# A gate projection's first two chunks made directly instead of by seven products

## The chip, the cores and the metric

One core of a Trainium2 chip runs the whole kernel. What counts is the device time of one execution in microseconds (us). Engines are named as in the profile: PE is TensorE, DVE is VectorE, ACT is ScalarE, POOL is GpSimd, SP is SyncE, which only issues transfers here.

## The reference, cut to what matters

An encoder block over 1024 tokens and 16 meta tokens of width 1024. The normalised input is projected by `w_in` to ten groups of columns. Two attention branches follow, each gated by `silu` of one group (`za`, `zb`) and projected by its own matrix. The last two groups, `ga` and `gb`, are 1024 columns each and are the subject here:

```python
proj = hn @ w_in[layer] + b_in[layer]
qa, ka, va, za, qb, kb, vb, zb, ga, gb = jnp.split(proj, SPLITS, axis=-1)
...
ya = (oa * jax.nn.silu(za)) @ w_out_a[layer]
yb = (ob * jax.nn.silu(zb)) @ w_out_b[layer]
mixed = jax.nn.sigmoid(ga) * ya + jax.nn.sigmoid(gb) * yb
h = h + rmsnorm(mixed @ w_out[layer], post_norm_g[layer])
```

All is float32. The kernel keeps that precision by splitting every operand into a high and a low part and adding three products: high by high, high by low, low by high.

## The kernel before

**Direct projection.** The normalised input lies transposed in four tiles: `hn00` and `hn01` are the high parts of the first and of the second half of the tokens, `hn10` and `hn11` the low parts. `proj` (lines 143 to 157) makes a chunk of 128 columns for two halves of 512 tokens: 24 matmuls of 128x512 for each half (8 slices of the width, three products), so 48 for a chunk. Its weights come by `load_w` (lines 121 to 141) in four pieces of two slices each: a load of 128 KB on SP's queue into a tile `wr`, a copy to the high part `wh` on POOL (line 139), and a subtraction for the low part `wl` on POOL (line 140).

**Seven products.** For `ga` and `gb` the input is cut into quarters, b11 and b21 (halves of the width for the first tokens), b12 and b22 (for the second tokens), and two chunks of columns are made together from seven products instead of eight (`seven`, lines 857 to 900). A product P1 to P7 is 12 matmuls of 128x512. P1, P2 and P3 use quarters as they are; P6, P5, P4 and P7 use the sums t2, t1, t4 and t3 of quarters. The weights of P5, P6, P3 and P7 are sums of weight blocks too, made on DVE (`total`, line 863, tiles `ws`). Every product's weights are split by `split` (lines 816 to 818): the high part on ACT, the low part on POOL. DVE adds the products up (line 897). The order is P1, P2, P6, P5, P3, P7, P4 (`SEVEN`).

**The sums of the input's quarters.** `combos` (lines 820 to 855) makes t1, t2, t4 and t3 in halves (f1, f2, f4, f3): two or three long DVE additions each, then a split, ACT for the high part and POOL for the low part. t3 is written over the quarter b12, so its split is a step of its own at the end of `combos`. Before that step eight steps run while the four chunks of `za` are projected directly (line 936), two with each chunk (lines 933 and 934). The last step is taken by `between`, ahead of P6 of the first pair of `ga`.

**Beside it.** `gate_a` (lines 905 to 914) gates the first branch in the `za` chunks: a sigmoid on ACT and DVE's lines 910 and 911, then a store of the result `ga_d`. `gate_b` (lines 916 to 923) gates the second branch, once for each pair of `ga`: loads of `zb_d` and `ob_d` on SP's queue, a sigmoid on ACT, two multiplications on DVE (lines 921 and 922) and a store on ACT's queue (line 923). Nine tiles of 128x1024, `TB`, are handed out in turn (`tl`, line 780) to all of these; the sums of quarters lie in them too until they are split. `wh` and `wl` have four buffers each, the weight blocks `wr4` of a pair three, the sums `ws` three, the product banks `pp` in PSUM six.

Each engine and each queue runs its instructions in order. A scheduler sets that order from the order of the code, from priorities and from its own estimates, so a step that is moved in the code moves its instructions on every engine.

Of the kernel before, what the change touches and what calls it, by code (L numbers as in the profile page):

```python
# [17 lines left out]
P = 128  # L18
# [3 lines left out]
MT = 16  # L22
# [8 lines left out]
QA, KA, VA, ZA, QB, KB, VB, ZB, GA, GB = 0, 512, 1024, 1536, 2048, 2560, 2688, 2816, 3328, 4352  # L31
# [9 lines left out]
QCH = ((16, 512), (528, 512))  # L41
# [32 lines left out]
def build(tc, ins, out, dbg=None, stop=None):  # L74
    with ExitStack() as ctx:
        _body(ctx, tc, ins, out, dbg or {}, stop)


def _body(ctx, tc, A, out, dbg, stop):
    nc = tc.nc  # L80
    pe, act, dve, pool, sp = nc.tensor, nc.scalar, nc.vector, nc.gpsimd, nc.sync
# [28 lines left out]
    def hslice(part, k, st, n):  # L110
        t = 0 if st < SPLIT else 1
        o = st - t * SPLIT
        return hn[part][t][:, k, o:o + n]

    def ld(o, i):
        return sp.dma_start(o, i)
# [4 lines left out]
    def load_w(src, kc=KC, into=None, whole=None):  # L121

        v = src.rearrange("(k p) c -> p k c", p=P)
        his, los = into or ([], [])
        if whole is not None:
            ld(whole, v)
        for k in range(0, kc, 2):
            if k % 4 == 0 and not into:
                his.append(wpool.tile([P, 4, P], F32R, tag="wh", name="wh", bufs=4))
                los.append(wpool.tile([P, 4, P], F32R, tag="wl", name="wl", bufs=4))  # L130
            o = slice(k % 4, k % 4 + 2)
            hi, lo = his[k // 4][:, o], los[k // 4][:, o]
            if whole is None:
                raw = (spare[0] if k % 8 == 6 and spare else wpool).tile([P, 2, P], F32, tag="wr", name="wr",
                                                                         bufs=1 if k % 8 == 6 and spare else 3)
                ld(raw, v[:, k:k + 2])
            else:
                raw = whole[:, k:k + 2]
            pool.tensor_scalar(hi, raw, 1.0, 1.0, ALU.mult, ALU.mult)  # L139
            pool.tensor_tensor(lo, raw, hi, ALU.subtract)  # L140
        return his, los

    def proj(col, chunks, evac, w=None, room=lambda: psmm.tile([P, 512], F32, tag="mm", name="mm")):

        hi, lo = w or load_w(A["w_in"][0, :, col:col + P])
        for st, n in chunks:
            ps = room()
            i = 0
            for w, part in ((hi, 0), (hi, 1), (lo, 0)):
                for k in range(KC):  # L150
                    pe.matmul(ps[:, :n], lhsT=w[k // 4][:, k % 4, :], rhs=hslice(part, k, st, n),  # L151
                              start=(i == 0), stop=(i == 3 * KC - 1))
                    i += 1
                yield
            with tc.high_priority(50):
                evac(ps, st, n, binT[:, col // P:col // P + 1])
            yield
# [10 lines left out]
    def run(*gens):  # L168
        for g in gens:
            for _ in g:  # L170
                pass
# [393 lines left out]
    if True:  # L565
        for c in range(4):
# [9 lines left out]
            for i in range(NB):  # L576
                n = int(BSTEPS[c][i])
# [202 lines left out]
    def tl():  # L780
        turn[0] += 1
        return TB[:, turn[0] % (KC + 1)]
# [3 lines left out]
    sg_d = dram.tile([KC, P, T], F32, name="sg_d")  # L786
    first = [True]

    def sigmoid(o, i, b=0.0):
        if first[0]:  # L790
            tc.keep_in_program_order(act.preload_act_table_set("sigmoid_and_others"))
        x = act.activation(o, i, AF.Sigmoid, bias=b)
        if first[0]:
            tc.keep_in_program_order(x)
            first[0] = False
# [24 lines left out]
    def combos():  # L820
        def halves(f):
            for j in range(2):
                k = slice(2 * j, 2 * j + 2)
                x = tl().rearrange("p (k t) -> p k t", k=2)
                f(x, k, j)
                yield
                xs[j] = x
        xs = [None, None]

        def f1(x, k, j):  # L830
            dve.tensor_tensor(x, b12[0][:, k], b11[0][:, k], sub)
            dve.tensor_tensor(x, x, b12[1][:, k], add)
            dve.tensor_tensor(x, x, b11[1][:, k], sub)
            split(t1, x, k)

        def f2(x, k, j):
            dve.tensor_tensor(x, b22[0][:, k], xs[j], sub)
            dve.tensor_tensor(x, x, b22[1][:, k], add)
            split(t2, x, k)

        def f4(x, k, j):
            dve.tensor_tensor(x, b21[0][:, k], xs[j], sub)
            dve.tensor_tensor(x, x, b21[1][:, k], add)
            split(t4, x, k)

        def f3(x, k, j):
            dve.tensor_tensor(x, b22[0][:, k], b12[0][:, k], sub)
            dve.tensor_tensor(x, x, b22[1][:, k], add)
            dve.tensor_tensor(x, x, b12[1][:, k], sub)
        for f in (f1, f2, f4, f3):  # L850
            yield from halves(f)

        for j in range(2):
            split(t3, xs[j], slice(2 * j, 2 * j + 2))
        yield
# [60 lines left out]
    def gate_b(j):  # L916
        z, o, s = tl(), tl(), tl()
        ld(z, zb_d[j])
        ld(o, ob_d[j])
        sigmoid(s, z)  # L920
        dve.tensor_tensor(z, z, s, ALU.mult)
        dve.tensor_tensor(z, z, o, ALU.mult)
        act.dma_start(gb_d[j], z)

    pieces = combos()
    for j in range(4):
# [4 lines left out]
        def evac(ps, st, n, b):  # L931
            if st == QCH[0][0]:
                next(pieces)
                next(pieces)
            ev((st - MT) // H, ps, b)
        run(proj(ZA + P * j, QCH, evac, **({"room": product} if j else {})))

    def gates(col, m, to, done=None, steps=SEVEN, between={}):

        col += P * m  # L940
        v = A["w_in"][0, :, col:col + 2 * P].rearrange("(j k p) c -> j p k c", p=P, j=2)
        a = {}
        for j in range(2):
            r = gp.tile([P, 4, 2 * P], F32, tag="wr4", name="wr4", bufs=3)
            ld(r, v[j])
            for i in range(2):
                a[f"a{i + 1}{j + 1}"] = r[:, :, i * P:i * P + P]
        count = [0, 0]

        def result(o, v, _):  # L950
            c, h = int(o[1]) - 1, int(o[2]) - 1
            sigmoid(to[c][:, h * H:h * H + H], v, binT[:, col // P + c:col // P + c + 1])
            count[c] += 1
            if done and count[c] == 2:
                done(c)
        run(seven(steps, a, IN, gp, gp, result, between=between))

    for p in range(4):
        s = [tl(), tl()]
        gates(GA, 2 * p, s, lambda c: act.dma_start(sg_d[2 * p + c], s[c]), between={} if p else {"P6": pieces})  # L960
        gate_b(p)
    for p in range(4):
        gates(GB, 2 * p, [TB[:, 2 * p + c] for c in range(2)], steps=LAST if p == 3 else SEVEN)
# [4 lines left out]
    room = [tp.tile([P, 2, T], F32, tag=f"t4{p}", name="room") for p in range(2)]  # L968
    room = [room[j // 2][:, j % 2] for j in range(4)]
# [164 lines left out]
```

## Time and profile before

| | |
|---|---|
| time, median of 3 runs | 901.52 us (899.78 to 901.94) |
| the profiled execution | 902.2 us |
| its span in the trace | 900.4 us |
| PE busy | 859.1 us, 95% |
| DVE busy | 672.2 us, 75% |
| ACT busy | 491.1 us, 55% |
| POOL busy | 381.2 us, 42% |

Times in the trace count from the span's start. The `za` chunks run from about 521 to 555, the pairs of `ga` from 555, the pairs of `gb` after them, then the output projections. A busy share is an average over stages with different limits; what a change in one stage is worth is read from that stage.

### The profile page before, as it was taken

To read this page: it belongs to the slowest core of one execution; us is meant where nothing else is said; L and a number is where in the kernel's file an instruction comes from. 1 tells how busy PE (TensorE), PEld (TensorE's weight loads), DVE (VectorE), ACT (ScalarE), POOL (GpSimd) and SP (SyncE) were. 2 spreads that over 40 slices of the span, in tenths; PEclk is the share of its full clock that TensorE was granted. 3 is DMA by queue.
4 is the path that set the end of the run, shared out by engine and by line. 5 is a ranking of instruction groups with operands and counts; after the bars stand their busy time and mean duration, and the time that the engine had idled before them with its cause. 6 is when DMAs were issued, how large, how long until landed. Compare 5 with 4: busy or idle time off the path is not lost.

```text
span 900.4 us, 13792 instructions
## 1 busy us (share of the span) xinstructions
PE 859.1 (95%) x4670; PEld 733.5 (81%) x4670; DVE 672.2 (75%) x1447; ACT 491.1 (55%) x977; POOL 381.2 (42%) x482
## 2 busy tenths in 40 slices
PE   5999999999999999999999998499999999999995
PEld 3898988888888998898888886388888888887785
DVE  6637577877989988997876599975444467959887
ACT  5536567676778878777766532344444531114442
POOL 6234444453121121221222198654454554935563
PEclk9999999999999999999999999699999999999998
DMA  8221111124121122030111153563511267221223
GB/s 282 79 63 33 51 48 44 67 73 114 47 63 54 48 72 68 25 95 24 48 65 48 47 195 123 172 210 140 179 56 47 102 210 250 68 103 47 94 96 139
DMA packets 64176, 85.32 MB, mean 95 GB/s; under 512 B 5233, under 2 KB 49279, under 8 KB 64106
## 3 DMA queue, kind: packets, MB, share of 16 engines
q1 hardware_dynamic: 56496, 59.75, 21.0%
q10 hardware_dynamic: 7578, 24.67, 8.0%
q8 instruction: 37, 0.61, 0.3%
q14 instruction: 33, 0.27, 0.1%
q0 software_dynamic: 32, 0.02, 0.0%
HBM read 60.11 MB, written 19.00 MB: 88 GB/s over the span
## 4 chain that ended last, share of the span: by engine, by line
PE 67%; DVE 17%; ACT 6%; issue 5%; POOL 3%; DMA 1%; DVEq 0%; ACTq 0%; POOLq 0%
PE mm L151 21%; PE pp L888 17%; PE pp L992 9%; PE pv L655 4%; PE s L613 3%; PE pT L643 3%; PE s L614 2%; PE pT L453 2%; POOL wl L818 2%; DVE sb L616 2%; DVE sb L626 2%; PE pv L471 2%; DVE TB L911 1%; ACT sb L625 1%; ACT sb L619 1%
## 5 line engine op out<-in xcount | busy, mean ns | idle before, releaser
L151 PE MATMUL mm<-hn,wh 128*128 128x512 f32 (+2 forms) x896 | 203.1, 356 | 0.9 <-DVE Q L333 0.9
L139 POOL TENSOR_SCALAR wh<-wr 128x256 fp32r<-128x256 f32 x124 | 63.8, 528 | 269.8 <-PE mm L151 241.4
L151 PEld LDWEIGHTS mm<-hn,wh 128*128 128x128 f32 x896 | 144.9, 191 | 16.8 <-issue 1.2
L140 POOL TENSOR_TENSOR wl<-wr,wh 128x256 fp32r<-128x256 f32 x124 | 109.5, 905 | 20.4 <-PE mm L151 18.4
L151 PE MATMUL mm<-hn,wl 128*128 128x512 f32 (+2 forms) x448 | 101.2, 353 | 0.0
L818 POOL TENSOR_TENSOR wl<-ws,wh 128x512 fp32r<-128x512 f32 x48 | 72.0, 1509 | 65.9 <-ACT wh L817 41.4
L619 ACT ACTIVATE sb<-sb,st 128x1040 f32<-128x1040 f32 x64 | 74.4, 1162 | 36.6 <-DVE st L616 36.0
L888 PE MATMUL pp<-t,wh 128*128 128x512 f32 (+1 forms) x296 | 73.4, 391 | 15.2 <-ACT wh L817 15.2
L151 PEld LDWEIGHTS mm<-hn,wl 128*128 128x128 f32 x448 | 73.5, 191 | 7.9 <-issue 0.4
L888 PE MATMUL pp<-hn,wh 128*128 128x512 f32 x320 | 79.8, 391 | 0.0
L888 PEld LDWEIGHTS pp<-t,wh 128*128 128x128 f32 x296 | 55.7, 192 | 27.5 <-ACT wh L817 16.0
L616 DVE CUSTOM_DVE_ANT_0 sb<-s,U,st 128x346 f32<-128x346 f32 x128 | 73.2, 573 | 5.9 <-PE mm L151 0.5
L897 DVE TENSOR_TENSOR c<-c,pp 128x512 f32<-128x512 f32 x70 | 47.3, 682 | 39.1 <-PE pp L888 38.2
L888 PEld LDWEIGHTS pp<-hn,wh 128*128 128x128 f32 x320 | 60.1, 188 | 13.2
L613 PE MATMUL s<-K,Q 128*128 128x346 f32 (+1 forms) x192 | 66.2, 347 | 0.4 <-DVE st L616 0.2
L614 PE MATMUL s<-K,Q 128*128 128x346 f32 (+1 forms) x192 | 61.1, 321 | 0.0
L626 DVE SCALAR_TENSOR_TENSOR sb<-sb,st 128x1040 f32<-128x1040 f32 x32 | 43.0, 1345 | 14.1 <-ACT sb L625 13.6
L438 POOL TENSOR_SCALAR sb<-sb,st 128x384 f32<-128x384 f32 (+2 forms) x64 | 35.2, 562 | 37.7 <-DVE st L436 37.7
L434 ACT ACTIVATE sb<-sb,st 128x385 f32<-128x385 f32 (+2 forms) x64 | 37.5, 588 | 22.1 <-DVE st L431 17.5
L817 ACT ACTIVATE wh<-ws 128x512 fp32r<-128x512 f32 x48 | 29.6, 625 | 34.9 <-PE pp L888 19.1
L431 DVE CUSTOM_DVE_ANT_0 sb<-s,TB,nsink 128x384 f32<-128x384 f32 (+2 forms) x64 | 35.4, 581 | 14.9 <-PE s L429 14.6
L645 DVE TENSOR_TENSOR al<-pT,ah 128x512 fp32r<-128x512 f32 x64 | 43.8, 686 | 1.8 <-ACT ah L644 0.9
(221 smaller groups left out, 1925.3 us busy)
## 6 DMA issues: line engine op xcount, KB each, us to landing
wr<-in_w_in_dram SPq DMA_DIRECT2D x96, 128.0 KB, 2.3
wr<-in_w_in_dram SPq DMA_DIRECT2D x16, 512.0 KB, 3.6
K<-K ACTq DMA_DIRECT2D x16, 260.0 KB, 3.6
xt<-in_x_dram SPq DMA_DIRECT2D x8, 512.0 KB, 5.1
sg_d<-TB ACTq DMA_DIRECT2D x8, 512.0 KB, 2.8
w<-in_w_out_dram SPq DMA_DIRECT2D x4, 1024.0 KB, 8.4
room<-sg_d SPq DMA_DIRECT2D x8, 512.0 KB, 4.5
fx<-in_x_dram SPq DMA_DIRECT2D x8, 512.0 KB, 4.6
```

Source lines behind the costliest of these rows:

```text
L139: pool.tensor_scalar(hi, raw, 1.0, 1.0, ALU.mult, ALU.mult)
L140: pool.tensor_tensor(lo, raw, hi, ALU.subtract)
L151: pe.matmul(ps[:, :n], lhsT=w[k // 4][:, k % 4, :], rhs=hslice(part, k, st, n), start=(i == 0), stop=(i == 3 * KC - 1))
L613: pe.matmul(s, lhsT=q, rhs=KH[:, m, o:o + n], start=True, stop=False)
L614: pe.matmul(s, lhsT=q, rhs=KL[:, m, o:o + n], start=False, stop=True)
L616: dve.tensor_tensor_reduce(out=sb[:, o:o + n], in0=s, in1=back(U, u0 + o, n), scale=-0.125, scalar=lim, op0=ALU.add, op1=ALU.min, accum_ou ...
L619: act.activation(sb, sb, AF.Exp, bias=st[:, m:m + 1], scale=-1.0, accum_out=st[:, 2 + m:3 + m])
L626: dve.scalar_tensor_tensor(sbs[0], sbs[0], st[:, 4:5], sbs[1], ALU.mult, ALU.add)
L818: lo_eng.tensor_tensor(t[1][:, k], x, t[0][:, k], sub)
L888: pe.matmul(x[n][:, cs], lhsT=w[:, k], rhs=b[n][part][:, k, cs], start=(i == 0), stop=(i == 11))
L897: dve.tensor_tensor(x[o][:, cs], *src, add)
L992: pe.matmul(py, lhsT=w[:, k, :], rhs=g[h][:, k], start=(i == 0), stop=(i == 11))
```

## The change

The first pair of `ga` is no longer made by seven products. Its two chunks are projected directly by `proj`, with a sigmoid from PSUM into the result tile. The last step of `combos`, the split of t3 over b12, is taken ahead of P3 of the second pair instead of P6 of the first. The other three pairs of `ga` and the four of `gb` stay as they are.

```diff
+    def gate_direct(col, to, done):
+
+        def evac(ps, st, n, b):
+            sigmoid(to[:, st - MT:st - MT + n], ps[:, :n], b)
+        run(proj(col, QCH, evac, room=product))
+        done()
+
     for p in range(4):
         s = [tl(), tl()]
-        gates(GA, 2 * p, s, lambda c: act.dma_start(sg_d[2 * p + c], s[c]), between={} if p else {"P6": pieces})
+        if p:
+            gates(GA, 2 * p, s, lambda c: act.dma_start(sg_d[2 * p + c], s[c]), between={"P3": pieces} if p == 1 else {})
+        else:
+            for c in range(2):
+                gate_direct(GA + P * c, s[c], partial(act.dma_start, sg_d[c], s[c]))
         gate_b(p)
```

POOL's order before, from t2's second half on: `t21` and `t41` are the low parts of t2 and t4, `hn11<-TB` is the low part of t3, `wl<-wr4` and `wl<-ws` are low parts of product weights.

```order
L818 TENSOR_TENSOR t21_6314<-TB_6298,t20_6313 128x1024
L818 TENSOR_TENSOR wl_6675<-wr4_6670,wh_6674 128x512
L818 TENSOR_TENSOR wl_6694<-wr4_6672,wh_6693 128x512
L818 TENSOR_TENSOR t41_6316<-TB_6298,t40_6315 128x1024 x2
L818 TENSOR_TENSOR hn11_89<-TB_6298,hn01_87 128x1024 x2
```

POOL's order now, from the same place up to the second direct chunk's third copy: `wh_6670` and `wh_6680` are the first chunk's weights, `wh_6743` and `wh_6753` the second's.

```order
L818 TENSOR_TENSOR t21_6314<-TB_6298,t20_6313 128x1024
L139 TENSOR_SCALAR wh_6670<-wr_6672 128x256
L139 TENSOR_SCALAR wh_6670<-wr_6676 128x256
L139 TENSOR_SCALAR wh_6680<-wr_6682 128x256
L140 TENSOR_TENSOR wl_6671<-wr_6672,wh_6670 128x256
L140 TENSOR_TENSOR wl_6671<-wr_6676,wh_6670 128x256
L140 TENSOR_TENSOR wl_6681<-wr_6682,wh_6680 128x256
L818 TENSOR_TENSOR t41_6316<-TB_6298,t40_6315 128x1024
L139 TENSOR_SCALAR wh_6680<-wr_6686 128x256
L140 TENSOR_TENSOR wl_6681<-wr_6686,wh_6680 128x256
L818 TENSOR_TENSOR t41_6316<-TB_6298,t40_6315 128x1024
L139 TENSOR_SCALAR wh_6743<-wr_6745 128x256
```

The chunks' copies and subtractions stand between the halves of t4; two more copies, four subtractions and one copy among them follow for the second chunk, then low parts of the second pair's weights with t3's halves between them.

ACT's order before, at the end of the `za` chunks: `c` are sigmoids of `gate_a`, `TB<-TB` is the sigmoid of `gate_b`, `wh_6721` is P6's weights.

```order
L913 DMA ga_d_6299<-TB_6298 128x1024
L792 ACTIVATE c_6636<-pp_6605,binT_78 128x512
L817 ACTIVATE hn01_87<-TB_6298 128x1024
L792 ACTIVATE TB_6298<-TB_6298 128x1024
L792 ACTIVATE c_6665<-pp_6640,binT_78 128x512
L817 ACTIVATE hn01_87<-TB_6298 128x1024
L895 ACTIVATE c_6691<-pp_6678 128x512
L817 ACTIVATE wh_6721<-ws_6719 128x512
```

ACT's order now, from the same store on: `pp_6690` is the first direct chunk's first half, `wh_6826` and `wh_6845` are P1's and P2's weights of the second pair.

```order
L913 DMA ga_d_6299<-TB_6298 128x1024
L792 ACTIVATE c_6636<-pp_6605,binT_78 128x512
L792 ACTIVATE TB_6298<-TB_6298 128x1024
L792 ACTIVATE c_6665<-pp_6640,binT_78 128x512
L913 DMA ga_d_6299<-TB_6298 128x1024
L792 ACTIVATE TB_6298<-pp_6690,binT_78 128x512
L923 DMA gb_d_6300<-TB_6298 128x1024
L817 ACTIVATE wh_6826<-wr4_6822 128x512
L817 ACTIVATE wh_6845<-wr4_6824 128x512
```

The copies of t3 are gone from here, and the store of `gate_b`'s product stands ahead of the weights of P1.

SP's order now, behind the last loads of `za`: `wr_67..` are pieces of the second direct chunk, `wr4_6987` is the third pair's second weight block.

```order
L116 DMA wr_6749<-in_w_in_dram 128x2x128
L116 DMA TB_6298<-ob_d_83 128x1024
L116 DMA wr_6755<-in_w_in_dram 128x2x128
L116 DMA TB_6298<-zb_d_85 128x1024
L116 DMA wr_6759<-in_w_in_dram 128x2x128
L116 DMA wr_7974<-in_w_out_b_dram 128x2x128
L116 DMA wr_7978<-in_w_out_b_dram 128x2x128
L116 DMA wr_8012<-in_w_out_b_dram 128x2x128
L116 DMA TB_6298<-ob_d_83 128x1024
L116 DMA TB_6298<-zb_d_85 128x1024
L116 DMA wr4_6987<-in_w_in_dram 128x4x256
L116 DMA TB_6298<-zb_d_85 128x1024
```

Before, the three `w_out_b` pieces came directly behind the last `za` piece, and the loads of `ob_d` and `zb_d` behind them; now the two last pieces of the second direct chunk stand behind such loads.

## Rows read from the trace of the kernel before

**Rows 1.** The page: the span, and busy time of each engine (share, instructions).

```profile
span 900.4 us, 13792 instructions
PE 859.1 (95%) x4670; PEld 733.5 (81%) x4670; DVE 672.2 (75%) x1447; ACT 491.1 (55%) x977; POOL 381.2 (42%) x482
```

**Rows 2.** Who waited for whom, PE: us in total, times, longest us.

```profile
PE pp L888 <- ACT wh L817: 15.6, 3, 14.7
...
PE pp L151 <- POOL wh L139: 0.6, 1, 0.6
```

**Rows 3.** PE in order of time: start us, us, what, count [idle before].

```profile
532.27 3.88 PE L151 MATMUL pp<-hn,wh 128*128 128x512 f32 x16
...
543.29 1.57 PE L151 MATMUL pp<-hn,wh 128*128 128x512 f32 x6
...
555.24 2.03 PE L888 MATMUL pp<-hn,wh 128*128 128x512 f32 x8
...
575.67 3.78 PE L888 MATMUL pp<-t,wh 128*128 128x512 f32 x8 [14.69 <-ACT wh L817]
...
580.96 2.02 PE L888 MATMUL pp<-t,wh 128*128 128x512 f32 x8
...
591.88 2.03 PE L888 MATMUL pp<-hn,wh 128*128 128x512 f32 x8
```

**Rows 4.** The chain that ended last, in order of time: start us, us, what.

```profile
561.14 2.27 DVE TB L847 x2
...
574.99 0.64 ACT wh L817
```

**Rows 5.** Stretches: busy us (count) of each engine, then PEclk, DMA share, GB/s.

```profile
562.00:563.00 1.00, 0.00 (x0) 0.00 (x0) 1.00 (x2) 0.24 (x1) 0.00 (x0) 1.00 1.04 422
...
564.00:565.00 1.00, 0.00 (x0) 0.00 (x0) 1.00 (x2) 0.00 (x0) 0.00 (x0) 0.50 0.11 37
...
579.00:580.00 1.00, 1.00 (x4) 0.81 (x3) 1.00 (x1) 0.00 (x0) 1.00 (x2) 0.50 0.45 94
```

**Rows 6.** POOL in order of time, as rows 3.

```profile
503.73 0.40 POOL L139 TENSOR_SCALAR wh<-wr 128x256 fp32r<-128x256 f32 x1 [0.85 <-DMA wr<-in_w_in_dram]
504.21 0.73 POOL L140 TENSOR_TENSOR wl<-wr,wh 128x256 fp32r<-128x256 f32 x1
...
546.55 3.38 POOL L818 TENSOR_TENSOR t<-TB,t 128x1024 fp32r<-128x1024 f32 x1
```

**Rows 7.** POOL by line (busy us, mean ns): 518.7 to 530.6, 530.6 to 546.5, 546.5 to 561.

```profile
L140 POOL TENSOR_TENSOR wl<-wr,wh 128x256 fp32r<-128x256 f32 x4 | 6.7, 1682 | 0.1
L139 POOL TENSOR_SCALAR wh<-wr 128x256 fp32r<-128x256 f32 x5 | 4.8, 979 | 14.3 <-PE mm L151 13.8 <-PE pp L151 0.4
...
L818 POOL TENSOR_TENSOR t<-TB,t 128x1024 fp32r<-128x1024 f32 x3 | 8.2, 2721 | 0.0
L140 POOL TENSOR_TENSOR wl<-wr,wh 128x256 fp32r<-128x256 f32 x4 | 5.1, 1286 | 0.1
L139 POOL TENSOR_SCALAR wh<-wr 128x256 fp32r<-128x256 f32 x4 | 3.5, 886 | 0.6 <-PE pp L151 0.4
...
L818 POOL TENSOR_TENSOR t<-TB,t 128x1024 fp32r<-128x1024 f32 x3 | 9.5, 3194 | 0.0
```

**Rows 8.** DVE: by line, 546.5 to 561, and one row in order of time.

```profile
L842 DVE TENSOR_TENSOR TB<-hn,TB 128x1024 f32<-128x1024 f32 x2 | 5.1, 2589 | 0.0
...
574.28 0.68 DVE L863 TENSOR_TENSOR ws<-ws,wr 128x512 f32<-128x512 f32 x1
```

**Rows 9.** ACT and SP in order of time; DMA issues, 519 to 585 (median us to landing).

```profile
553.30 1.06 ACT L817 ACTIVATE t<-TB 128x1024 fp32r<-128x1024 f32 x1 [5.68 <-DVE TB L843]
...
563.86 6.88 SPq L116 DMA_DIRECT2D TB<-zb_d  x2
...
TB<-zb_d SPq DMA_DIRECT2D x3, 512.0 KB, 6.7
wr<-in_w_in_dram SPq DMA_DIRECT2D x5, 128.0 KB, 2.1
```

## Prediction

> **What bounds the kernel now.** I read the page's head first: TensorE is busy for 95% of a span of 900.4 us [rows 1], so only its idle time and its matmul count can pay. The table of who waited for whom shows one idle stretch that matters: one wait of 14.7 us of PE at line 888 for ACT's line 817 [rows 2]. PE in order of time shows where [rows 3]: P1 and P2 of the first pair of gate chunks start at 555.24, and P6 starts at 575.67 after 14.69 us without work, so P2 ended at 560.98. The chain of waits says why [rows 4]: from 561.14 on VectorE makes the last quarter sum (f3, lines 847 to 849), then what is queued behind it, and only then the pair's weight sums (line 863); ACT's copy of P6's weights starts at 574.99. P6 needs nothing of f3; its sums stand behind f3 in VectorE's order.
>
> The stretch costs more than its idle time. TensorE's granted clock is still 1.00 up to 563, is 0.50 from 564 on and still is up to 580 [rows 5]: the lower of the two levels, 1.2 instead of 2.4 GHz. So P6 takes from 575.67 to 580.96, 5.29 us, where the next four products take 10.92, or 2.73 each [rows 3]: 2.56 us lost. The first pair is done at 591.88 [rows 3]; from there on PE is without a gap worth naming, so what the change moves that point by is what the span moves by.
>
> **What it removes and adds on PE.** Gone are the first pair's seven products of 12 matmuls (84); instead two chunks of 48 (96) run directly. A direct chunk's price is in the trace: the chunk from 532.27 to 543.29 is 48 such matmuls with no wait, 11.02 us, or 0.230 each [rows 3]. Two take 22.04, so without any wait PE would be done with the pair at 555.24 + 22.04 = 577.28 instead of 591.88: a gain of 14.6. That is 14.69 of idle time [rows 3] and 2.56 of slow clock, less 12 matmuls at 0.230 (2.8), to within 0.2. VectorE loses four sums and seven additions of the pair, none of which PE waits for any more.
>
> **What it adds on POOL, and who waits.** Each direct chunk's weights come in four pieces, each a copy (line 139) and a subtraction (line 140) on POOL; before, ACT made the high parts of P1 and P2 and POOL two short subtractions. POOL is free of the t2 sums at 549.93 in the trace [rows 6]. After the change its order is three copies, three subtractions, then the first half of t4's low part, and only behind that the fourth copy of the first chunk. PE starts on the first chunk at 555.24, and after six matmuls (1.4 us, at 556.6) it needs that fourth copy. Prices when VectorE streams beside POOL: copies 0.89 to 0.98, subtractions 1.29 to 1.68, a half of t4 2.72 to 3.19 [rows 7]; the ends are means of three stretches. So the copy is done at 549.93 + 4x0.89 + 3x1.29 + 2.72 = 560.1 at the low end and 549.93 + 4x0.98 + 3x1.68 + 3.19 = 562.1 at the high end. I take the middle, 561.1, since VectorE's work beside it is between that of the two stretches: PE waits 4.5 us (3.5 to 5.5). The same order already made PE wait once, 0.6 us [rows 2].
>
> The second chunk's fourth copy comes after one subtraction, the other half of t4, three copies and three subtractions, and itself: 4x1.29 + 2.72 + 4x0.89 = 11.4 to 4x1.68 + 3.19 + 4x0.98 = 13.8 us more, so at 571.5 to 575.9, middle 573.7. PE gets there by itself from 561.1 with 42 matmuls (9.7) and six more (1.4): 572.2. After the fourth copy 42 matmuls remain, 9.7 us.
>
> Does the clock fall in the wait of 4.5? The trace has it at 1.00 from 562 to 563 and at 0.50 from 564 to 565 of a wait that began at 560.98 [rows 5], so I take it that it falls within the 4.5; the price would again be 2.56, and PE would get to the second chunk's fourth copy at 574.7. PE leaves the direct chunks at max(573.7, 574.7) + 9.7 = 584.4, against 583.4 without the fall: the clock and POOL's lateness lie over each other and are not added. Low end: 571.5 + 9.7 = 581.2; high end: 575.9 + 9.7 = 585.6. I take 584.3. The gain is 591.88 - 584.3 = 7.6 us, between 6.3 and 10.7.
>
> **What else moves.** SP: the third piece of the second chunk stands behind a load of ob_d that waits for the first half of t4 (about 560), the fourth behind a load of zb_d, which the trace issues at 563.86; pieces land in 2.1 us [both rows 9], so in time for copies at about 568 and 573.
>
> ACT: the store of gate_b's product (line 923) now stands ahead of the copy of the second pair's P1 weights. It waits for VectorE: f3 from about 561, six operations that alone take 1.13 each [rows 4], to 568, or at 2.59 [rows 8] to 576.6; behind it seven smaller ones, some 6 us alone (0.68 each for the short sums [rows 8]). I take 580, plus 1 us for store and copy: 581, some 3 us ahead of 584.3. This wait costs nothing as long as POOL is late, and becomes the limit if POOL is not.
>
> The last split, t3, writes over b12, which the direct matmuls read to their end. It moves from P6 of the first pair to P3 of the second. After PE's end E, POOL has a low part of weights (twice the size of the 0.73 of [rows 6], so 1.46), half of t3 (2.72 to 3.19, as t4 [rows 7]) and P5's low part (1.46): E + 5.6 to 6.1. P5's sum tile is then free, P7's sum (0.68 [rows 8]) ends by E + 6.8, and SP can load the third pair's second weight block and behind it gate_b's next zb_d, which lands in 6.7 us [rows 9]: E + 13.5. Two ACT operations of at most 1.06 us, the longer copies' price [rows 9], stand between that and the copy of P4's weights: E + 15.6, against a need at E + 6x2.73 = E + 16.4. It is hidden by 0.8 us.
>
> **Sum.** PE's end of the pair moves from 591.88 to 584.3, -7.6; the rest is covered. The profiled execution's time is 902.2, 1.8 over its span, and 0.7 above the median of 901.52. The forecast is 901.52 - 7.6 = 893.9.
>
> **The rivals.** *POOL keeps up.* Were its prices those of POOL alone, 0.40 and 0.73 [rows 6], the fourth copy would come at 557.5, behind the half of t4, whose copy on ACT ends at 554.36 [rows 9]; PE would wait 0.9 us, the clock would stay, and PE would be done at 578.2: 13.7 us gained, 887.8. For it: the weights' loads are early enough. Against: VectorE has no idle time in this stretch, and both window means show POOL slowed.
>
> *POOL and VectorE take full turns.* If each POOL instruction beside VectorE first waited for one whole sum of 1.13 us [rows 4], a copy would take 0.40 + 1.13 = 1.53, a subtraction 0.73 + 1.13 = 1.86 and a half of t4 its 3.19: the first chunk's fourth copy at 549.93 + 4x1.53 + 3x1.86 + 3.19 = 564.8, the second's 4x1.86 + 3.19 + 4x1.53 = 16.8 later at 581.6, PE done at 591.3: 0.6 us gained, 900.9. Against: VectorE streamed in the first of the three stretches too, and a copy took 0.98 and a subtraction 1.68 there [rows 7], not these prices. The Trainium skill (SBUF — State Buffer, section "SBUF: two separate sides") has the rule behind this rival: a GpSimd operation and one of VectorE with two SBUF inputs exclude each other for the whole of an instruction. The trace agrees in direction, and only the full turn at every instruction is not borne out.
>
> *The gain is spent a second time.* The wait for P4's weights opens if zb_d's load lands more than 0.8 us later than reckoned, and then costs one for one; with POOL at its high end too (6.3 gained), 4 us of it leave 2.3, about 899.2. Against: 6.7 us is already a loaded figure.
>
> *Slower than before.* SP's queue is the place: the second chunk's fourth piece stands behind zb_d's load, which waits until gate_a's store of the chunk before has landed, which waits for VectorE's line 911. From an issue of that load after 571 on (563.86 in the trace) PE waits us for us; at 582 the piece is copied at about 585, PE ends the chunk at 594.7, 2.8 later than before: 904.3. Against: VectorE's line 911 there precedes f3 and is not moved back by the change.
>
> *It doesn't do what it says*: the two chunks' matmuls stand right behind line 936's last chunk on PE, so this has no chance of its own.
>
> **How the numbers follow.** Chances: forecast 0.62, POOL keeps up 0.18, full turns 0.08, spent again 0.05, slower 0.07. A measurement of this kernel can tell about 0.3%, 2.7 us, from no change. Faster by more is the first two, 0.80; within it the next two, 0.13; slower 0.07. The range reaches from 887.8 of the first rival to 898, past the high end's 895.2 to where the cases of small gain begin: 888 to 898.
>
> **What would show it.** Right: two waits of PE at line 151 for POOL's line 139 at about 556.6 and 573, together 4 to 7 us; a granted clock of 0.50 for some us after the first; P1 of the second pair at 584; no wait of PE at line 888 over 1 us after it. Wrong: waits under 1 us (then POOL's prices were too high), or a wait at line 888 for ACT's line 817 at P1, P4 or the third pair's P1 (then the gate_b chain is the limit).

## The result, and the profile after

The changed kernel takes 894.99 us (median of 4 runs, 893.79 to 895.12), the kernel before 901.70 us on the same chip (median of 4, 899.78 to 901.94). The ratio is 0.993, with a 95% interval of 0.9914 to 0.9946: faster, by 0.5 to 0.9%. The medians lie 6.7 us apart. The forecast was 893.9 us, with a range of 888 to 898.

The page's head of the changed kernel, which answers to [rows 1]:

```profile
span 893.3 us, 13803 instructions
...
PE 862.0 (96%) x4682; PEld 735.8 (82%) x4682; DVE 664.9 (74%) x1436; ACT 486.0 (54%) x969; POOL 384.7 (43%) x491
```

PE has 12 instructions more, DVE 11 fewer, POOL nine more; the span is 7.1 us shorter. Who PE waited for, changed kernel (us in total, times, longest us), answering to [rows 2]:

```profile
PE pp L151 <- POOL wh L139: 4.3, 2, 3.9
...
PE pp L888 <- ACT wh L817: 0.9, 2, 0.5
```

The wait of 14.7 us at line 888 is gone; one of 3.9 at line 151, for POOL's copies, has come. PE of the changed kernel in order of time (start us, us, what, count, [idle before]), answering to [rows 3]; the rows at 543.96, 555.74, 573.64 and 584.66 begin the last `za` chunk, the first and the second direct chunk, and P1 of the second pair:

```profile
543.96 1.57 PE L151 MATMUL pp<-hn,wh 128*128 128x512 f32 x6
...
555.74 1.57 PE L151 MATMUL pp<-hn,wh 128*128 128x512 f32 x6
561.17 4.63 PE L151 MATMUL pp<-hn,wh 128*128 128x512 f32 x10 [3.86 <-POOL wh L139]
565.60 2.74 PE L151 MATMUL pp<-hn,wl 128*128 128x512 f32 x8
568.19 3.80 PE L151 MATMUL pp<-hn,wh 128*128 128x512 f32 x16
...
573.64 3.88 PE L151 MATMUL pp<-hn,wh 128*128 128x512 f32 x16
...
584.66 2.03 PE L888 MATMUL pp<-hn,wh 128*128 128x512 f32 x8
```

The stage is read from the first matmul of the last `za` chunk, because the profiled executions of this study differ by up to 2.7 us in their first 100 us, before any of this. From there to P1 of the second pair it was 591.88 - 543.29 = 48.59 us [rows 3] and is 584.66 - 543.96 = 40.70: 7.89 shorter. From P1 to the end of the span it was 900.4 - 591.88 = 308.52 and is 893.3 - 584.66 = 308.64. So all of the gain lies in this stage, and nothing is given back later. It adds up from rows: the wait fell from 14.69 to 3.86 (10.83), 12 matmuls at 0.230 were added (-2.76), and the slow clock costs about what it did: 18 matmuls from 561.17 to 568.19 take 7.02 us where 18 x 0.230 = 4.14 would do, 2.9 against 2.56 before. That makes 7.7.

The granted clock (the column behind the five engines; stretches in us, columns as in [rows 5]):

```profile
560.00:561.00 1.00, 0.00 (x0) 0.00 (x0) 1.00 (x2) 0.00 (x0) 1.00 (x1) 0.68 0.36 70
561.00:562.00 1.00, 0.83 (x2) 0.74 (x3) 1.00 (x1) 0.00 (x0) 0.92 (x2) 0.50 0.71 270
```

The wait began at 557.3; the clock fell to 1.2 GHz in its last part, from about 560.3 on, and PE worked at that level until about 567.

What PE waited for is in POOL's rows, and the reason for their length stands beside them in DVE's. Both in order of time; lines 139 and 140 are the chunks' copies and subtractions, line 818 the first half of t4, line 843 the last sum of f4, lines 910 and 911 gate_a's:

```profile
550.42 4.05 POOL L139 TENSOR_SCALAR wh<-wr 128x256 fp32r<-128x256 f32 x3
554.44 2.59 POOL L140 TENSOR_TENSOR wl<-wr,wh 128x256 fp32r<-128x256 f32 x3
556.99 2.79 POOL L818 TENSOR_TENSOR t<-TB,t 128x1024 fp32r<-128x1024 f32 x1
559.75 1.37 POOL L139 TENSOR_SCALAR wh<-wr 128x256 fp32r<-128x256 f32 x1
...
566.06 4.05 POOL L139 TENSOR_SCALAR wh<-wr 128x256 fp32r<-128x256 f32 x3
570.07 3.02 POOL L140 TENSOR_TENSOR wl<-wr,wh 128x256 fp32r<-128x256 f32 x3
573.07 1.49 POOL L139 TENSOR_SCALAR wh<-wr 128x256 fp32r<-128x256 f32 x1
```

```profile
551.46 2.75 DVE L843 TENSOR_TENSOR TB<-TB,hn 128x1024 f32<-128x1024 f32 x2
554.13 1.40 DVE L910 SCALAR_TENSOR_TENSOR c<-pp,binT,c 128x512 f32<-128x512 f32 x2
```

While DVE makes its long sums (line 843: two inputs in SBUF), POOL's copy takes 4.05 / 3 = 1.35 us and DVE's sum 1.38. While DVE reads PSUM (line 910), it takes 0.70 for one; POOL's three subtractions beside it and the short line 911 take 2.59 / 3 = 0.86 each on average.

### The profile page after: what moved, and what is told of

It reads as the page before. It is cut to its first block, busy times and chain, and to the rows that moved or that the text cites. A ratio compares the mean times of both kernels' runs of the same rounds, so it can differ in the third digit from the quotient of the medians.

```text
span 893.3 us, 13803 instructions
## 1 busy us (share of the span) xinstructions
PE 862.0 (96%) x4682; PEld 735.8 (82%) x4682; DVE 664.9 (74%) x1436; ACT 486.0 (54%) x969; POOL 384.7 (43%) x491
## 4 chain that ended last, share of the span: by engine, by line
PE 68%; DVE 11%; POOL 7%; issue 6%; ACT 6%; DMA 2%; DVEq 0%; ACTq 0%; POOLq 0%
PE mm L151 21%; PE pp L888 17%; PE pp L1003 9%; PE pv L655 4%; PE s L613 3%; PE pp L151 3%; PE pT L643 2%; PE s L614 2%; POOL wl L140 2%; DVE sb L616 2%; PE pT L453 2%; DVE sb L626 2%; POOL t L818 2%; PE pv L471 2%; ACT sb L625 1%
## 5 line engine op out<-in xcount | busy, mean ns | idle before, releaser
L139 POOL TENSOR_SCALAR wh<-wr 128x256 fp32r<-128x256 f32 x132 | 75.0, 582 | 268.8 <-PE mm L151 241.4
L140 POOL TENSOR_TENSOR wl<-wr,wh 128x256 fp32r<-128x256 f32 x132 | 115.7, 898 | 20.6 <-PE mm L151 18.4
L818 POOL TENSOR_TENSOR wl<-ws,wh 128x512 fp32r<-128x512 f32 x44 | 64.7, 1478 | 58.1 <-ACT wh L817 37.8
L888 PE MATMUL pp<-hn,wh 128*128 128x512 f32 x288 | 71.8, 391 | 0.0
L888 PE MATMUL pp<-t,wh 128*128 128x512 f32 (+1 forms) x272 | 65.6, 383 | 0.5 <-ACT wh L817 0.5
L897 DVE TENSOR_TENSOR c<-c,pp 128x512 f32<-128x512 f32 x63 | 42.5, 682 | 30.3 <-PE pp L888 29.2
L888 PEld LDWEIGHTS pp<-hn,wh 128*128 128x128 f32 x288 | 54.1, 188 | 11.9
L888 PEld LDWEIGHTS pp<-t,wh 128*128 128x128 f32 x272 | 50.1, 188 | 11.0 <-ACT wh L817 0.9
L151 PE MATMUL pp<-hn,wh 128*128 128x512 f32 x160 | 41.0, 409 | 4.3 <-POOL wh L139 4.3
```

The costliest lines, as they stand in the source:

```text
L818: lo_eng.tensor_tensor(t[1][:, k], x, t[0][:, k], sub)
L888: pe.matmul(x[n][:, cs], lhsT=w[:, k], rhs=b[n][part][:, k, cs], start=(i == 0), stop=(i == 11))
```

## The experiments

Unless said otherwise an edit is made to the changed kernel. Each ratio is against runs of the kernel before on the same chip: median 902.13 us for the first four kernels, 901.19 for the last three.

**Does POOL's lateness or PE's idle clock cost the time?** Seventeen matmuls that nobody reads are put on PE ahead of the first direct chunk, about the length of the wait.

```diff
             for c in range(2):
+                if c == 0:
+                    idle = psmm.tile([P, 512], F32, tag="mm", name="idle")
+                    for i in range(NDUMMY):
+                        pe.matmul(idle, lhsT=b11[0][:, 0, 0:P], rhs=b11[0][:, i % 4], start=(i == 0), stop=(i == NDUMMY - 1))
                 gate_direct(GA + P * c, s[c], partial(act.dma_start, sg_d[c], s[c]))
```

> The changed kernel with 17 extra matmuls of 128x512 (3.9 us at full clock, into a bank nobody reads) put on PE ahead of the first direct chunk, so that PE works while it would have waited 3.86 us for POOL's fourth copy. Theory (POOL's supply of the second chunk's weights sets the end of the two chunks, and the slow clock after the first wait lies over it): the clock stays at 1.00, the wait at the first chunk is under 0.5 us, a wait of about 2.4 us appears at the second chunk's fourth copy, and the two chunks end within 0.6 us of before: 894.6, between 894.0 and 895.3. Rival (the slow clock after the wait adds its 2.6 us to the path): 892.4.

Measured: 895.08 us (892.77 to 895.9), ratio 0.9921 (0.9907 to 0.9935). PE of this kernel in order of time; line 975 is the idle work, all other lines are one further down than in the changed kernel:

```profile
554.76 4.09 PE L975 MATMUL idle<-hn 128*128 128x512 f32 x17
558.69 4.14 PE L152 MATMUL pp<-hn,wh 128*128 128x512 f32 x16
...
573.72 3.84 PE L152 MATMUL pp<-hn,wh 128*128 128x512 f32 x10 [2.18 <-POOL wh L140]
```

The first chunk now runs without a wait, its 16 matmuls in 4.14 us instead of being held until 561, and PE then waits 2.18 us before the second chunk's fourth copy, which it met in the changed kernel with 0.5 us to spare. POOL's last copy ends 30.7 us after the last `za` chunk's start (573.67 - 542.96), and 30.6 in the changed kernel: PE's early arrival brings next to nothing, so in the changed kernel the slow clock and POOL's lateness lie over each other, as the sum had it. One part of the expectation did not hold: the clock did not stay up. It fell once PE had gone on (the stretches in the last section), and the 18 matmuls from 573.72 to 579.57 took 5.85 us, 1.7 more than at full clock. Behind POOL's last copy nothing hides that: by the trace the stage is 585.02 - 542.96 = 42.06 us, 1.36 longer than in the changed kernel, which the medians don't show.

**Does it matter where POOL makes the halves of t4?** Both halves are held on POOL, once behind the first chunk's four pieces, once behind all eight. The text of the edit is the same but for one number (`lows[-5]` in the first, `lows[-1]` in the second). In both, the loads and splits of the two chunks' weights also stand together in the code, ahead of the matmuls of either. The cut leaves out where `lows` and `x4` are filled and where `gate_direct` takes `w`.

```diff
+        for x, k in x4:
+            act.activation(t4[0][:, k], x, AF.Copy)
+            y = pool.tensor_tensor(t4[1][:, k], x, t4[0][:, k], sub)
+            tc.add_manual_dep(y.ins, lows[-1].ins.name, mybir.DependencyInfo(
+                mybir.DependencyClass.NoSync, mybir.DependencyReason.DATA), reason="weights first")
+        yield
...
+            w = [load_w(A["w_in"][0, :, GA + P * c:GA + P * c + P]) for c in range(2)]
+            next(pieces)
             for c in range(2):
-                gate_direct(GA + P * c, s[c], partial(act.dma_start, sg_d[c], s[c]))
+                gate_direct(GA + P * c, s[c], partial(act.dma_start, sg_d[c], s[c]), w[c])
```

> The changed kernel with both halves of t4's low part moved on POOL behind all four pieces of the first direct chunk; the second chunk's pieces still stand behind them. Theory (POOL's total work up to the second chunk's fourth copy is the limit): PE's first wait shrinks from 3.9 to 1 to 2 us, the clock stays at 1.00, a second wait of 4 to 6 us comes at the second chunk, the end of the chunks stays: 894.5, between 893.5 and 895.5. Rival (the place of t4 ahead of the first chunk's fourth piece is the limit): 891 to 892.

Measured behind the first four pieces: 894.94 us (894.27 to 895.43), ratio 0.9924 (0.9912 to 0.9936). PE, second chunk:

```profile
572.17 4.63 PE L152 MATMUL pp<-hn,wh 128*128 128x512 f32 x10 [3.70 <-POOL wh L140]
```

Of the wait at the first chunk 0.57 is left, but it has moved to the second, where two waits of 0.6 stand ahead of the 3.70. POOL's last copy ends 30.7 us after the last `za` chunk's start (572.12 - 541.43), so no earlier than in the changed kernel. The clock falls in the 3.70, and now nothing hides that: the 18 matmuls from 572.17 to 579.13 take 6.96 us instead of 4.14, and by the trace the stage is 584.58 - 541.43 = 43.15 us, 2.45 longer. The time of the runs is the same as that of the changed kernel within their intervals; why the 2.45 do not show there stays open.

> The changed kernel with both halves of t4's low part moved on POOL behind all eight pieces of both direct chunks. Theory (POOL's order is what is left of the wait): first wait 1 to 2 us, second wait under 1.5 us, chunks end some 5 us earlier: 890, between 888.5 and 891.5. Rival (gate_b's store ahead of P1's weights on ACT is the next limit at once, since the ob_d load waits for t4's tile): a wait of PE for ACT at P1 of 2 us or more, 892 to 894.

Measured behind all eight: 890.5 us (889.79 to 892.37), ratio 0.9882 (0.9867 to 0.9898). PE, where line 896 is the products and lines 818 and 819 are the splits of their weights:

```profile
555.83 2.59 PE L152 MATMUL pp<-hn,wh 128*128 128x512 f32 x10 [0.57 <-POOL wh L140]
...
576.58 2.03 PE L896 MATMUL pp<-hn,wh 128*128 128x512 f32 x8
...
590.84 1.20 PE L896 MATMUL pp<-hn,wl 128*128 128x512 f32 x4 [1.03 <-POOL wl L819]
...
598.37 2.11 PE L896 MATMUL pp<-hn,wh 128*128 128x512 f32 x8 [0.82 <-ACT wh L818]
```

Only 0.57 is left of the wait, the clock stays up, and the stage is 576.58 - 541.89 = 34.69 us, 6.0 shorter than in the changed kernel. Of that, 2.8 are given back later (888.0 - 576.58 = 311.42 to the end of the span, against 308.64), most of it in two waits that the changed kernel hasn't (1.03 and 0.82). So the wait came from t4's halves standing between the chunks' pieces, 2.8 and 3.35 us of POOL's time in the changed kernel that no product needed before P4, which starts at 594.60 here.

**Could the seven products have been kept?** In the kernel before, f3 is moved out of the way instead: its two steps no longer run in the last `za` chunk but ahead of P3 of the first pair.

```diff
-            if st == QCH[0][0]:
+            if st == QCH[0][0] and j < 3:
                 next(pieces)
                 next(pieces)
...
-        gates(GA, 2 * p, s, lambda c: act.dma_start(sg_d[2 * p + c], s[c]), between={} if p else {"P6": pieces})
+        gates(GA, 2 * p, s, lambda c: act.dma_start(sg_d[2 * p + c], s[c]), between={} if p else {"P3": pieces})
```

> The kernel before, with seven products for all four pairs, but with the last quarter sum f3 not made with the fourth za chunk: it is made with the split of t3 ahead of P3 of the first pair, so that the sums of P5's and P6's weights stand ahead of f3 on VectorE. Theory (the wait of 14.7 us came from VectorE's order, f3 ahead of P6's sums): PE's wait ahead of P6 falls from 14.7 to 3 us or less, a new wait of 3 to 6 us comes ahead of P7, which needs t3, and the first pair ends 9 to 13 us earlier than before: 889 to 893. Rival (VectorE and POOL simply have too much work in this stretch, in whatever order): the first pair ends within 4 us of before: 898 to 902.

Measured: 896.48 us (896.31 to 899.45), ratio 0.995 (0.9936 to 0.9963), between the two expectations. PE:

```profile
564.84 3.78 PE L888 MATMUL pp<-t,wh 128*128 128x512 f32 x8 [3.32 <-ACT wh L817]
...
578.39 1.66 PE L888 MATMUL pp<-hn,wh 128*128 128x512 f32 x6 [1.35 <-ACT wh L817]
...
583.26 1.19 PE L888 MATMUL pp<-hn,wl 128*128 128x512 f32 x4 [1.47 <-POOL wl L818]
...
588.63 2.02 PE L888 MATMUL pp<-hn,wh 128*128 128x512 f32 x8
```

The wait before P6 fell from 14.69 [rows 3] to 3.32, so DVE's order did make most of it. But f3 then comes back as waits before and in P7, where t3 is used (1.35, 1.00 for t3 itself, 1.47), the clock falls in the 3.32 too (eight matmuls in 3.78 us) and once more at P4's start (eight in 3.57), and the first pair ends at 588.63. The profiled run was the slowest of the six; by it the stage, 44.65 us, is 3.94 shorter than before, half of what the change brings. By the runs it is more than half, 0.5% against 0.7%, and the two intervals overlap. So f3's place alone brings between half and most of the gain. That the rest comes from the direct chunks, which need no sums while f3 is made, is argued from the order and not shown.

**What if POOL has fewer instructions?** The high parts of the two chunks' weights are copied on ACT; POOL only subtracts.

```diff
-            pool.tensor_scalar(hi, raw, 1.0, 1.0, ALU.mult, ALU.mult)
+            if hi_eng is None:
+                pool.tensor_scalar(hi, raw, 1.0, 1.0, ALU.mult, ALU.mult)
+            else:
+                act.activation(hi, raw, AF.Copy)
...
-        run(proj(col, QCH, evac, room=product))
+        run(proj(col, QCH, evac, load_w(A["w_in"][0, :, col:col + P], hi_eng=act), room=product))
```

> The changed kernel, with the high parts of the two direct chunks' weights copied on ACT instead of POOL, which then only subtracts for them; the subtractions still stand around the two halves of t4. Theory (PE waited because POOL had eight instructions between t2 and the first chunk's fourth copy): with four copies (1.35 to 1.40 each) off POOL, ACT's copies come before PE reaches them, and no wait at the first chunk's sixth matmul is left. POOL makes three subtractions, both halves of t4 (2.79 and 3.35), then the fourth subtraction at about 563; PE needs that low part some 23 matmuls after its start, at about 561, so a wait of about 2 us is left, now before the low parts, and P1 of the second pair starts at about 580 instead of 584.7: 890 to 891 us. Rival (the bound is VectorE's or the loads' pace, not POOL's number of instructions): P1 stays at 583 to 585 and the time at 894 to 896.

Measured: 888.48 us (887.93 to 890.56), ratio 0.9864 (0.9844 to 0.9885), the lowest ratio of this study, though its interval overlaps that of t4's halves behind all eight. PE, where lines 142 and 143 are the copies on ACT and the subtractions on POOL, and line 891 the products:

```profile
559.58 0.73 PE L154 MATMUL pp<-hn,wl 128*128 128x512 f32 x2 [0.83 <-POOL wl L143]
...
567.78 2.59 PE L154 MATMUL pp<-hn,wh 128*128 128x512 f32 x10 [0.61 <-ACT wh L142]
...
577.52 2.03 PE L891 MATMUL pp<-hn,wh 128*128 128x512 f32 x8
```

The stage is 577.52 - 541.68 = 35.84 us, and no wait comes after it: 886.1 - 577.52 = 308.58 to the end, the same as before. The expectation had the stage right: from the changed kernel's start of the last `za` chunk at 543.96 to its P1 at about 580 is 36.0. Within it, a wait of 2 us was expected, where 0.83 and, not expected, 0.61 for an ACT copy came. The runs lie 1.5 to 2.5 us below the expected 890 to 891, and this stage explains only 0.2 of that; the rest stays open. POOL's rows against DVE's are also the plainest in the study, each pair of rows from the same stretch (POOL's lines 143 and 821 are the chunks' subtractions and the halves of t2 and t4; DVE's lines 845 and 846 are f4's sums):

```profile
544.79 3.39 POOL L821 TENSOR_TENSOR t<-TB,t 128x1024 fp32r<-128x1024 f32 x1
548.13 5.08 POOL L143 TENSOR_TENSOR wl<-wr,wh 128x256 fp32r<-128x256 f32 x3
```

```profile
545.83 3.43 DVE L845 TENSOR_TENSOR TB<-hn,TB 128x1024 f32<-128x1024 f32 x1
549.18 3.44 DVE L846 TENSOR_TENSOR TB<-TB,hn 128x1024 f32<-128x1024 f32 x2
```

A half takes 3.39 on POOL and the sum beside it 3.43 on DVE; a subtraction takes 1.69 and the sum beside it 1.72. The two engines go in step, one instruction of each in turn.

**What sets the price of POOL's copies?** f3's three additions are replaced by one copy on ACT, so what this kernel uses as t3 is not the sum.

```diff
-            dve.tensor_tensor(x, b22[0][:, k], b12[0][:, k], sub)
-            dve.tensor_tensor(x, x, b22[1][:, k], add)
-            dve.tensor_tensor(x, x, b12[1][:, k], sub)
+            act.activation(x, b22[0][:, k], AF.Copy)
```

> The changed kernel with the last quarter sum f3 left out: its three additions on VectorE for each half are replaced by one copy on ACT, so what is used as t3 is not the sum. The question is what sets the price of POOL's copies and subtractions. Theory (a POOL instruction beside an addition of VectorE whose two inputs lie in SBUF waits for a turn): with no such additions from about 557 on, the second chunk's copies take about 0.4 and its subtractions about 0.73 us instead of 1.35 and 1.0, the second half of t4 less than its 3.35, and the second chunk's fourth copy ends some 5 us earlier against the last za chunk's start. PE's first wait, which ends at 561, gets shorter by at most 1.5 us. Rival (the prices are POOL's own here, by the length of the instruction or by the loads it follows): copies stay at 1.3 to 1.4 and subtractions at 0.9 to 1.0.

Measured: 890.34 us in one run. POOL of this kernel, second chunk, and behind it DVE (line 908 reads PSUM, line 919 is gate_b's multiplication):

```profile
562.49 1.21 POOL L139 TENSOR_SCALAR wh<-wr 128x256 fp32r<-128x256 f32 x2
...
564.69 2.12 POOL L140 TENSOR_TENSOR wl<-wr,wh 128x256 fp32r<-128x256 f32 x3
568.84 1.29 POOL L139 TENSOR_SCALAR wh<-wr 128x256 fp32r<-128x256 f32 x1 [2.03 <-DMA wr<-in_w_in_dram]
```

```profile
562.99 0.74 DVE L908 SCALAR_TENSOR_TENSOR c<-pp,binT,c 128x512 f32<-128x512 f32 x1
...
568.65 1.22 DVE L919 TENSOR_TENSOR TB<-TB 128x1024 f32<-128x1024 f32 x1 [4.19 <-ACT TB L792]
```

With the long sums gone, the first three copies take 0.60, 0.60 and 0.53 and the subtractions 0.71; the one copy that meets a long multiplication of DVE (568.65) takes 1.29 again. So the theory holds on the price. It missed on the time: the second chunk's fourth copy ends at 570.1, 28.3 us after the last `za` chunk's start against 30.6 in the changed kernel, so 2.4 us earlier and not 5, because its piece of weights was now what came last (2.03 of waiting for a DMA). Its load was issued at 565.45, and SP's queue (us in total, times, longest us) had waited for POOL just before:

```profile
SPq L116 <- POOL wl L140: 1.1, 1, 1.1
```

The tile `wr` has three buffers here (line 135), so a chunk's fourth piece needs that of its first, and POOL's first subtraction of the chunk, from 564.69 on, gave it back. zb_d's load, ahead of it on the queue, had been issued at 563.95 already. So this is not the mechanism of the rival *slower than before*, and it shows what limits the stage next: the fourth copy can't come before POOL's first subtraction of its chunk and the load behind that, 3.4 us here (565.45 to 568.84). The first wait is not a clean test here: in this kernel the first chunk's fourth copy stands ahead of t4's first half.

**Can the wait that came later, with t4's halves behind all pieces, be avoided?** In the kernel with t4's halves behind all pieces, t3's halves are also held behind P3's low part and taken ahead of P7.

```diff
-            gates(GA, 2 * p, s, lambda c: act.dma_start(sg_d[2 * p + c], s[c]), between={"P3": pieces} if p == 1 else {})
+            gates(GA, 2 * p, s, lambda c: act.dma_start(sg_d[2 * p + c], s[c]), between={"P7": pieces} if p == 1 else {})
...
+            if t is t3:
+                tc.add_manual_dep(y.ins, lows[-1].ins.name, mybir.DependencyInfo(
+                    mybir.DependencyClass.NoSync, mybir.DependencyReason.DATA), reason="weights first")
```

> The kernel with t4's halves behind all pieces (t4_last), and besides t3's two halves, which stood ahead of P3's low part in the second pair and made PE wait 1.03 us there, held on POOL behind P3's low part and taken in the code ahead of P7 instead of P3. Theory (that wait is POOL's order alone): the wait at P3's low part goes, nothing later takes its place, and the time is 889 to 890 us, about 1 us below t4_last. Rival (the chain from b12's last reader through t3, the sums and the next pair's loads has no slack): the wait comes back before P7 or before P1 of the third pair, and the time is 890.5 us or more.

Measured: 891.45 us (890.35 to 892.53), ratio 0.989 (0.9873 to 0.9907). The theory fell: the wait of 1.03 at P3 is gone, and P7 waits instead (line 902 is the products, line 819 POOL's part of the splits):

```profile
592.34 0.73 PE L902 MATMUL pp<-hn,wh 128*128 128x512 f32 x2 [0.33 <-POOL hn L819]
594.04 1.20 PE L902 MATMUL pp<-hn,wl 128*128 128x512 f32 x4 [0.97 <-POOL wl L819]
```

POOL's 5 us for t3, which may not begin before the direct matmuls have ended (at about 576.7 here), made PE wait in both places of the second pair that were tried, ahead of P3 and of P7.

## Why the prediction was right, step by step

**What bounded the kernel.** Right. Only the one wait mattered, and the rest after P1 did not move: it is 308.52 and 308.64 us. That P6's sums waited behind f3 in DVE's order is shown by the kernel that moves f3, where the wait falls from 14.69 to 3.32.

**The first chunk's fourth copy.** Forecast 10.1 to 12.2 us after POOL is free, middle 11.15; measured 561.12 - 550.42 = 10.70. The sum was right, its terms were not. Four copies took 1.35 to 1.37 each, not 0.89 to 0.98; three subtractions 0.86 each, not 1.29 to 1.68; the half 2.79. The errors are +1.7 for the copies and -1.9 for the subtractions against the middle values, and they cancel, which is luck. The means of [rows 7] were over copies and subtractions that stood beside all sorts of DVE instructions; the price belongs to what DVE does at the moment, not to the kind of POOL instruction. Alone, a copy takes 0.40 and a subtraction 0.73 [rows 6]; beside DVE's long sums 1.35 and 1.69, which is 0.95 and 0.96 more. A half is 3.39 there and 2.4 where no long sum runs beside it.

**Full turns.** I gave this rival 0.08 and argued that a copy took 0.98 and a subtraction 1.68 in a stretch where DVE streamed. That argument read a mean wrongly. POOL's first rows of that stretch, in the kernel before (518.7 to 530.6), and the row where DVE's long sums begin in it:

```profile
518.77 1.21 POOL L139 TENSOR_SCALAR wh<-wr 128x256 fp32r<-128x256 f32 x2 [13.83 <-PE mm L151]
519.95 1.37 POOL L139 TENSOR_SCALAR wh<-wr 128x256 fp32r<-128x256 f32 x1
521.29 5.06 POOL L140 TENSOR_TENSOR wl<-wr,wh 128x256 fp32r<-128x256 f32 x3
```

```profile
519.64 2.75 DVE L831 TENSOR_TENSOR TB<-hn,hn 128x1024 f32<-128x1024 f32 x2
```

The 1.68 of a subtraction was the full turn: 0.73 and 0.95. The copies' 0.98 was the mean of two that began ahead of the long sums (0.60 each), two beside them (1.37, at 519.95 and 526.32) and one that POOL began after an idle time, in the middle of a sum (0.92, at 529.80). Where DVE makes sums of two SBUF inputs and POOL's instructions follow each other without a gap, the turn is full at every instruction, with 0.95 us for DVE instead of my 1.13. The Trainium skill's rule (SBUF — State Buffer, section "SBUF: two separate sides") is borne out: POOL's and DVE's rows beside each other have the same length (3.39 and 3.43, 1.69 and 1.72). The rival's time, 900.9, was still far off, because only part of DVE's instructions are such sums: with 0.95 at every one of the eight instructions the fourth copy would have come 4 x 1.35 + 3 x 1.69 + 3.39 = 13.9 us after POOL is free, not 10.70.

**The second chunk and the clock.** Forecast 11.4 to 13.8 us after the first chunk's fourth copy; measured 574.56 - 561.12 = 13.4, at the high end, since f3 ran beside most of it. The clock fell in the wait, as taken, and cost 2.9 instead of 2.56. PE came to the second chunk's seventh matmul at 573.64 + 1.4 = 575.0, the copy was done at 574.56: no second wait. My list of what would show it named two waits of 4 to 7 us together, where one of 3.86 came, and that was a slip, since my own sum had PE arrive later than the copy (574.7 against 573.7). So was its low end of 581.2: with the clock fallen, PE itself would have been at that copy only at 560.1 + 11.1 + 2.56 = 573.8 and done at 583.5, so the most it could gain was 8.4 and not 10.7. By rows the two ends are 0.5 us apart, and the dummy matmuls show the second wait as soon as PE is earlier.

**The end.** P1 at 584.66, forecast 584.3. The start of the stage lies 0.67 later than before, so the stage itself gained 7.89 against a forecast of 7.6.

**What else moves.** The prediction had SP's fourth piece wait behind zb_d's load, issued at 563.26 here. It waited for POOL much longer, for a buffer of `wr` that the chunk's first subtraction (from 570.07) gave back:

```profile
SPq L116 <- POOL wl L140: 7.1, 1, 7.1
```

It was issued at 570.83, and its copy could start at 573.07, when POOL came to it: in time, with next to nothing to spare. I had gate_b's store at 581, 3 us ahead of the need; the rows of ACT put it at 576.81, because gate_b's last multiplication on DVE (line 922) ended at 576.8, and P1's weights were ready 7 us early. P4's chain, forecast to be hidden by 0.8 us, was hidden by more:

```profile
576.81 0.34 ACTq L923 DMA_DIRECT2D gb_d<-TB  x1
577.20 1.15 ACT L817 ACTIVATE wh<-wr 128x512 fp32r<-128x512 f32 x2 [1.00 <-DVE TB L922]
...
593.40 1.06 ACT L792 ACTIVATE TB<-TB 128x1024 f32<-128x1024 f32 x1 [3.26 <-DMA TB<-zb_d]
...
596.59 0.62 ACT L817 ACTIVATE wh<-wr 128x512 fp32r<-128x512 f32 x1
```

P4's weights are ready at 597.2 and its first matmul starts at 601.13: 3.9 us of room. That the chain zb_d, sigmoid, weights exists is in the rows; its price was over-sized by 3.1 us.

**The rivals.** *POOL keeps up* fell by the wait of 3.86, but its time, 887.8, is what a kernel reaches whose POOL does keep up (888.48 with the copies on ACT). *Spent again* and *slower* did not come. Of the second one's chain the kernel without f3 shows a piece: zb_d's load waited 3.8 us there for gate_a's store, but the weights behind it then waited for POOL, so the queue did not set their time.

## What to carry to other kernels

When one engine's instructions are priced from a trace, price them by what runs beside them at that moment, not by the mean of a stretch: POOL copies cost 0.40 us alone and 1.35 in turns with long sums, and a mean over both fits neither. When a wait is replaced by work that another engine has to feed, look at that engine's order for long instructions that nobody needs yet: two t4 halves behind the copies, or the copies on an engine with idle time, gave another 0.5 to 0.7% beyond the change. When only the place of a wait is changed and not its cause, it comes back at the next place, as with t4's halves between the two chunks and with t3's ahead of P7.

## What the runs showed of the hardware

The granted clock did not follow the length of a wait alone. It fell in the waits of 3.86 us (the changed kernel), 3.70 (t4 between the chunks) and 3.32 (f3 moved). After the wait of 2.18 in the kernel with dummy matmuls it was still 1.00 when PE went on at 573.72, and fell afterwards, while PE was working (columns as in [rows 5]):

```profile
574.00:575.00 1.00, 1.00 (x5) 0.78 (x5) 1.00 (x2) 0.00 (x0) 0.80 (x1) 0.85 0.01 2
575.00:576.00 1.00, 1.00 (x3) 0.79 (x3) 1.00 (x2) 0.00 (x0) 0.00 (x0) 0.50 0.98 373
```

After a wait of 2.63 in the kernel without f3 it stayed at 1.00. What decides between the two stays open; no run here tells it apart. What a fall costs depends on where it lies: ahead of POOL's last copy it was hidden but for some 0.5 us (the changed kernel, 2.9 us); behind it, it made the stage longer (1.7 with the dummy matmuls, 2.8 with t4 between the chunks).

The turns between POOL and DVE cost both sides. DVE's long sum takes 1.21 us while POOL has nothing to do (line 852 of the kernel with the copies on ACT); it took 1.38 beside a copy, 1.72 beside a subtraction and 3.43 beside a half.
